# Norm 2's vectors loaded after gate/up's second chunk, and the cross heads' probabilities turned directly behind their scaling

## The chip, the cores and the metric

The kernel runs on one NeuronCore of a Trainium2 chip. The metric is device time in microseconds, the median of several executions of the same program. Before the change three executions took 380.92, 380.79 and 378.37 us, so the median is 380.79 us. One more execution was recorded by the profiler, and every row below is from it: it took 380.38 us.

## The reference

One decoder layer on 256 tokens of width 1024, in float32: a pooling mixer beside causal attention, then cross-attention of four heads of width 256 into 256 memory tokens, then a SwiGLU feed-forward of width 2816. A layer norm stands behind each of the three parts. What the change touches is the cross-attention and its norm:

```python
def memory_cross_attention(h, mem, w_xq, w_xkv, w_xo):
    q = (h @ w_xq).reshape(B_, S_, XATTN_HEADS, XATTN_HEAD_DIM)
    kv = mem @ w_xkv
    ...
    s = jnp.einsum('bshd,bmhd->bhsm', q, k, ...) * (XATTN_HEAD_DIM ** -0.5)
    p = jax.nn.softmax(s, axis=-1)
    o = jnp.einsum('bhsm,bmhd->bshd', p.astype(v.dtype), v).reshape(B_, S_, D)
    return o @ w_xo
...
    h = layer_norm(DEEPNORM_ALPHA * h + memory_cross_attention(h, mem, w_xq[l], w_xkv[l], w_xo[l]),
                   ln2_g[l], ln2_b[l])
```

## The kernel before

Every weight matrix is read once, in pieces of 512 KB, by one stream (class `Stream`). A piece lands in one of seven `raw` buffers, ACT copies it to a rounded tile `hi` (L99), and DVE subtracts to get the remainder `lo` (L100). TensorE then forms each product from three matmuls, hi·hi, hi·lo and lo·hi (L256 to L258, L274). All loads are issued from SP's queue in program order, and a load waits until the `raw` buffer that it fills has been split. `ws.before(number, load)` puts another load into that queue just ahead of piece `number`; norm 2's two vectors, `g` and `b` (512 KB each, one row of 4 KB repeated over 128 partitions, L224), stand there ahead of the first and the third piece of gate/up's first chunk.

The order of the instructions on each engine is the order in which the Python code is written. Generators such as `do_xq(h)` (the query product of head h, 16 steps of three matmuls) are advanced by `run(gen, n)`, and other calls are put between.

For each cross head h the path is:

- `xscores(h)`: the scores on TensorE into tile `xs` in PSUM; the row maximum (L440, DVE), the exponentials (L429, ACT), and the scaling by the sums (L434 and L436, DVE) give the probabilities `xpr`.
- `xprobs_out(h)`: DVE turns 32x32 blocks of `xpr` into a tile that is also called `xs` (L340), and POOL's queue issues one DMA of 256 KB that writes it to a DRAM tile `xd` (L343).
- `xprobs_in(h)`: POOL's queue issues four DMAs of 64 KB (L351) that read `xd` back, block rows exchanged, into `xr`. They wait for the write to land.
- `xprobs_split(h)`: ACT and DVE split `xr` into hi and lo, tile `xst` (L319, L320).
- `xattend(h)`: TensorE multiplies `xst` with the values `xv` into tile `xo` (L256 to L258).

Head 3 is turned on TensorE instead (`xprobs_pe`). The pieces below call these steps out(h), in(h) and split(h).

The tiles `xs` (of L340), `xr` and `xst` share one tag of the pool `small`, with three buffers. A new tile of the tag takes a buffer whose former tile is finished with by the code written so far, and its first writer then waits for that tile's last readers and writers:

```python
st = sp.tile([P, 4, n, 32], F32, name=f"{name}s", tag="pair", bufs=3)       # xs, in turned()
raw = sp.tile([P, 4, n, 32], F32, name=f"{name}r", tag="pair", bufs=3)      # xr, in landed()
st = sp.tile([P, 2, 2, S], F32R, name="xst", tag="pair", bufs=3)            # xst, in xprobs_split()
```

Behind the fourth head's scores comes the output product of the cross-attention (`project(c_xo, ...)`, tile `acc`), norm 2, and the gate/up product (tile `pg`).

Of the kernel before, what the change touches and what calls it, by code (L numbers as in the profile page):

```python
# [125 lines left out]
def decoder_layer(  # L126
# [18 lines left out]
    def bank(name):  # L145
        return pb.tile([P, 512], F32, tag="b", name=name)
# [5 lines left out]
    ws = Stream(nc, wp)  # L152
# [28 lines left out]
    c_gu = [ws.add(w_gu[c], 4) for c in range(NFC)]  # L181
# [39 lines left out]
    def load_norm(tag, i, v):  # L221
        def load():
            gb[tag, i] = nmp.tile([P, D], F32, tag=tag, name=f"{tag}{i}")
            nc.sync.dma_start(gb[tag, i], v[None, :].to_broadcast([P, D]))  # L224
        return load
# [1 line left out]
    ws.before(c_v[3][0], load_mem)  # L227
    ws.before(c_xk[1][0], load_pool)
    ws.before(c_mix[3][0], load_x)
    ws.before(c_gu[0][0], load_norm("g", 2, ln2_g))  # L230
    ws.before(c_gu[0][2], load_norm("b", 2, ln2_b))
    ws.before(c_dn[4][0], load_norm("g", 3, ln3_g))
    ws.before(c_dn[6][0], load_norm("b", 3, ln3_b))

# [18 lines left out]
    def three(ps, w, y, start, stop, part=False):  # L253

        (wa, wb), (ya, yb) = w, y
        nc.tensor.matmul(ps, wa, ya, start=start, stop=False, skip_group_check=part)  # L256
        nc.tensor.matmul(ps, wa, yb, start=False, stop=False, skip_group_check=part)  # L257
        nc.tensor.matmul(ps, wb, ya, start=False, stop=stop, skip_group_check=part)  # L258

    def pair(hl, *ix):  # L260
        return hl[0][ix], hl[1][ix]
# [48 lines left out]
    def run(gen, n=None):  # L310

        while n is None or n > 0:
            if next(gen, gen) is gen:
                return False
            n = None if n is None else n - 1
        return True
# [18 lines left out]
    def turned(blocks, n, name, queue=nc.sync):  # L335

        st = sp.tile([P, 4, n, 32], F32, name=f"{name}s", tag="pair", bufs=3)
        for at, src in blocks:
            m = src.shape[1]
            nc.vector.transpose(st[:, :, at:at + m, :].rearrange("p j m b -> p m j b"),  # L340
                                src.rearrange("p m (j b) -> p m j b", b=32))
        via = hp.tile([P, 4, n * 32], F32, name=f"{name}d")
        queue.dma_start(via, st.rearrange("p j m b -> p j (m b)"))  # L343
        return via

    def landed(via, n, name, queue=nc.sync, raw=None):

        if raw is None:
            raw = sp.tile([P, 4, n, 32], F32, name=f"{name}r", tag="pair", bufs=3)
        for j in range(4):  # L350
            queue.dma_start(raw[32 * j:32 * (j + 1)].rearrange("p i m b -> p i (m b)"),  # L351
                              via[:, j, :].rearrange("(i a) r -> a i r", i=4))
        return raw
# [72 lines left out]
    def exps(dst, src, mx, sign=1.0):  # L426
        sm = sp.tile([P, 2], F32, name="sm", bufs=6)
        for j in range(2):
            nc.scalar.activation(dst[:, j, :], src[:, j, :], AF.Exp, bias=mx[:, j:j + 1], scale=sign,  # L429
                                 accum_out=sm[:, j:j + 1])  # L430
        return sm

    def scaled(dst, sm):
        nc.vector.reciprocal(sm, sm)  # L434
        for j in range(2):
            nc.vector.tensor_scalar(dst[:, j, :], dst[:, j, :], sm[:, j:j + 1], None, op0=OP.mult)  # L436

    def negmax(src):
        mx = sp.tile([P, 2], F32, name="mx", bufs=6)
        nc.vector.tensor_reduce(mx, src, op=OP.max, axis=AX.X, negate=True)  # L440
        return mx
# [287 lines left out]
    def do_xq(h):  # L729
        ps = (bank if h == 0 else accbank)("pxq").rearrange("p (f t) -> p f t", f=2)  # L730
        yield from proj_t([ps[:, f, :] for f in range(2)], c_xq[h], h1T)
        xqT[h] = [sp.tile([P, 2, S], F32R, name=f"xq{i}", tag="pr", bufs=PR_BUFS) for i in range(2)]
        split_scaled(*xqT[h], ps, 256 ** -0.5)

    def xscores(h):
        ps = bank("xs").rearrange("p (t s) -> p t s", t=2)
        for t in range(T):
            for kk in range(2):
                three(ps[:, t, :], pair(xqT[h], ALL, kk, slice(t * P, (t + 1) * P)), pair(xkT, ALL, 2 * h + kk),
                      kk == 0, kk == 1)  # L740
        pr = sp.tile([P, 2, T, P], F32, name="xpr", tag="pr", bufs=PR_BUFS)
        by_t = pr.rearrange("p s t b -> p t s b")
        scaled(by_t, exps(by_t, ps.rearrange("p t (s b) -> p t s b", s=2), negmax(ps)))
        xpr[h] = pr

    def xprobs_out(h):
        turnsx[h] = turned([(0, xpr[h].rearrange("p s t b -> p (s t) b"))], 4, "x", nc.gpsimd)

    def xprobs_in(h):
        turnsx[h] = landed(turnsx[h], 4, "x", queue=nc.gpsimd)  # L750

    def xprobs_split(h):
        raw = turnsx[h].rearrange("p i m b -> p m i b")
        st = sp.tile([P, 2, 2, S], F32R, name="xst", tag="pair", bufs=3)
        xpt[h] = st[:, 0], st[:, 1]
        split(*[x.rearrange("p s (t i b) -> p (s t) i b", t=T, i=4) for x in xpt[h]], raw)
# [18 lines left out]
    xq = [do_xq(h) for h in range(XH)]  # L775
    run(xq[0])
    run(xq[1], 5)
    xscores(0)
    run(xq[1])
    xprobs_out(0)  # L780
    run(xq[2], 5)
    xscores(1)
    xprobs_in(0)
    run(xq[2])
    xprobs_out(1)
    run(xq[3], 5)
    xscores(2)
    xprobs_in(1)
    xprobs_split(0)
    run(xq[3])  # L790
    xprobs_out(2)

    h2 = ap.tile([P, T, D], F32, tag="a8", name="h2")
    xo = project(c_xo, lambda k: (oT[0][:, k], oT[1][:, k]), 4)
# [177 lines left out]
```

## Time and profile before

| what | value |
|---|---|
| median of three executions | 380.79 us (378.37 to 380.92) |
| profiled execution | 380.38 us |
| its span, first to last instruction | 378.6 us |
| mean granted TensorE clock | 0.993 |
| PE busy | 367.7 us (97%) |
| DVE busy | 262.2 us (69%) |
| ACT busy | 177.4 us (47%) |
| POOL busy | 34.7 us (9%) |
| DMA | 84.52 MB, mean 223 GB/s |

The profiler numbers everything from the span's start; 1.8 us of the profiled execution lie around the span. PE is TensorE's matmuls and PEld its weight loads, DVE is VectorE, ACT ScalarE, POOL GpSimd, SP SyncE. A bracket behind a row of the timeline gives how long the engine was idle ahead of it and what ended that. The granted clock is a share of TensorE's 2.4 GHz: 1.00, or 0.50 for 1.2 GHz. From issue to landing of a DMA is counted from the start of the instruction that issues it.

### The profile page before, as it was taken

Reading aid. Unit: us, or ns where it says so; the run is one execution under the profiler, and the core shown is the slowest. Engines: PE = TensorE matmul, PEld = TensorE weight load, DVE = VectorE, ACT = ScalarE, POOL = GpSimd, SP = SyncE. Lnnn points to the kernel's source line nnn. Section 1 sums busy time; section 2 is a strip of 40 time slices with the busy share of each in tenths; the row PEclk is TensorE's granted clock in tenths of the full one; section 3 lists DMA queues with packets and bytes.
Section 4 is the critical chain, followed back from the end, with each engine's and each line's share of the span. In section 5 each row is a group of like instructions: output and inputs, shape, how many; then the busy total and the mean of one; then the engine's idle time right before and its main releaser. Section 6 shows DMA issues by size and latency. Waiting matters only on the chain.

```text
span 378.6 us, 5525 instructions
## 1 busy us (share of the span) xinstructions
PE 367.7 (97%) x2024; PEld 317.6 (84%) x2024; DVE 262.2 (69%) x388; ACT 177.4 (47%) x259; POOL 34.7 (9%) x66
## 2 busy tenths in 40 slices
PE   9999999999999999899999999999999999999992
PEld 8997998997878999788878888888888888888881
DVE  4778899974698877465889765666665666353275
ACT  4756775653152944354138445454545454434000
POOL 1000157140110002320100000000000000000000
PEclk9999999999999999899999999999999999999998
DMA  7998699799337998544107998787879977730011
GB/s 236 412 412 298 190 341 307 261 251 367 124 111 234 392 312 265 150 155 161 56 2 264 353 308 256 243 238 250 237 230 316 279 241 251 206 106 0 0 51 62
DMA packets 32539, 84.52 MB, mean 223 GB/s; under 512 B 4096, under 2 KB 12160, under 8 KB 32384
## 3 DMA queue, kind: packets, MB, share of 16 engines
q1 hardware_dynamic: 30224, 79.05, 63.7%
q0 software_dynamic: 1712, 4.72, 4.2%
q10 hardware_dynamic: 576, 0.39, 0.3%
q8 instruction: 16, 0.26, 0.3%
q14 instruction: 11, 0.09, 0.1%
HBM read 76.81 MB, written 7.34 MB: 222 GB/s over the span
## 4 chain that ended last, share of the span: by engine, by line
PE 89%; DVE 4%; DMA 3%; issue 1%; ACT 1%; POOL 0%; SPq 0%; DVEq 0%
PE pg L258 10%; PE pg L257 10%; PE pg L256 10%; PE acc L256 9%; PE acc L257 9%; PE acc L258 9%; PE pxk L274 6%; PE pqk L392 6%; PE pxq L274 3%; PE pu L274 3%; PE xv L256 2%; PE xv L258 2%; PE xv L257 2%; DMA w61r<-in_w_gu 1%; PE pv L256 1%
## 5 line engine op out<-in xcount | busy, mean ns | idle before, releaser
L623 POOL TENSOR_TENSOR rs<-rs,mhalf 128x1 f32<-128x1 f32 x6 | 5.4, 897 | 231.4 <-DVE rs L622 231.4
L832 ACT ACTIVATE sg<-pg 128x256 f32<-128x256 f32 x22 | 8.4, 383 | 12.9 <-PE pg L258 12.8
L612 DVE SCALAR_TENSOR_TENSOR r<-h,acc 128x256 f32<-128x256 f32 (+1 forms) x10 | 5.1, 520 | 10.9 <-PE acc L258 10.9
L833 DVE TENSOR_TENSOR sg<-sg,pg 128x256 f32<-128x256 f32 x22 | 9.3, 421 | 4.0 <-ACT sg L832 2.6
L429 ACT ACTIVATE pr<-pr,mx 128x128 f32<-128x128 f32 (+1 forms) x16 | 7.1, 444 | 8.3 <-DVE mx L460 8.3
L351 POOL DMA_DIRECT2D pt<-pd x16 | 8.8, 555 | 6.6 <-DMA pd<-ps 4.1
L319 ACT CAST h2Th<-tp 128x512 fp32r<-128x512 f32 x4 | 2.3, 587 | 13.5 <-PE tp L330 13.4
L615 DVE BATCH_NORM_STATS2 st<-r 128x6 f32<-128x512 f32 (+1 forms) x14 | 8.1, 580 | 0.5
L320 DVE TENSOR_TENSOR gTl<-gr,gTh 128x512 fp32r<-128x512 f32 x11 | 7.5, 686 | 1.2 <-ACT gTh L319 1.2
L429 ACT ACTIVATE xpr<-xs,mx 128x256 f32<-128x256 f32 x8 | 3.7, 471 | 9.1 <-DVE mx L440 9.1
L319 ACT CAST gTh<-gr 128x512 fp32r<-128x512 f32 x11 | 6.8, 616 | 2.2 <-DMA gr<-gd 2.2
L628 DVE SCALAR_TENSOR_TENSOR r<-r,mv,g 128x512 f32<-128x512 f32 x11 | 7.8, 743 | 0.0
L340 DVE STREAM_TRANSPOSE gs<-sg 128x512 f32<-128x512 f32 x11 | 7.8, 705 | 0.0
L351 POOL DMA_DIRECT2D xr<-xd x12 | 6.5, 550 | 13.1 <-DMA w61r<-in_w_gu 5.4
L343 POOL DMA_DIRECT2D pd<-ps x4 | 2.5, 614 | 51.0 <-DVE ps L340 50.7
L256 PE MATMUL xo<-xst,xv 128*128 128x256 f32 x16 | 5.0, 314 | 1.5 <-ACT xst L319 1.5
L436 DVE TENSOR_SCALAR pr<-pr,sm 128x128 f32<-128x128 f32 (+1 forms) x16 | 6.2, 425 | 0.3
L434 DVE RECIPROCAL sm<-sm 128x2 f32<-128x2 f32 x12 | 2.0, 163 | 5.5 <-ACT xpr L429 4.4
L320 DVE TENSOR_TENSOR oTl<-xo,oTh 128x512 fp32r<-128x512 f32 x4 | 2.8, 692 | 4.2 <-ACT oTh L319 4.2
L634 DVE SCALAR_TENSOR_TENSOR h<-r,rs,b 128x512 f32<-128x512 f32 x8 | 5.6, 744 | 0.0
L319 ACT CAST oTh<-xo 128x512 fp32r<-128x512 f32 x4 | 2.3, 587 | 6.9 <-PE xo L258 6.9
L257 PE MATMUL xo<-xst,xv 128*128 128x256 f32 x16 | 5.1, 317 | 0.3 <-DVE xst L320 0.3
(1092 smaller groups left out, 1414.3 us busy)
## 6 DMA issues: line engine op xcount, KB each, us to landing
gd<-gs SPq DMA_DIRECT2D x11, 256.0 KB, 4.9
gr<-gd SPq DMA_DIRECT2D x44, 64.0 KB, 4.7
pd<-ps POOLq DMA_DIRECT2D x4, 384.0 KB, 4.9
pt<-pd POOLq DMA_DIRECT2D x16, 96.0 KB, 8.1
g<-in_ln_g SPq DMA_DIRECT2D x3, 512.0 KB, 6.1
b<-in_ln_b SPq DMA_DIRECT2D x3, 512.0 KB, 6.7
wr<-in_w_qkv SPq DMA_DIRECT2D x5, 256.0 KB, 5.4
mr<-in_mem_t SPq DMA_DIRECT2D x1, 1024.0 KB, 11.7
```

Of the source, the lines that this page charges most:

```text
L256: nc.tensor.matmul(ps, wa, ya, start=start, stop=False, skip_group_check=part)
L257: nc.tensor.matmul(ps, wa, yb, start=False, stop=False, skip_group_check=part)
L258: nc.tensor.matmul(ps, wb, ya, start=False, stop=stop, skip_group_check=part)
L274: nc.tensor.matmul(pss[f], w[:, s], y, start=k == 0 and f == 0 and n == 0, stop=k == KD - 1 and n == 2, skip_group_check=True)
L319: nc.scalar.copy(h, ps)
L320: nc.vector.tensor_sub(l, ps, r32(h))
L351: queue.dma_start(raw[32 * j:32 * (j + 1)].rearrange("p i m b -> p i (m b)"), via[:, j, :].rearrange("(i a) r -> a i r", i=4))
L392: nc.tensor.matmul(qk[i][:, f, :], w[:, c * P:(c + 1) * P], y, start=k == 0 and f == 0 and w is hi and y is x_hi, stop=k == KD - 1 and w i ...
L429: nc.scalar.activation(dst[:, j, :], src[:, j, :], AF.Exp, bias=mx[:, j:j + 1], scale=sign, accum_out=sm[:, j:j + 1])
L615: nc.vector.bn_stats(self.st[:, self.n, :], self.r[:, c0:c1])
L832: nc.scalar.activation(sg, ps[:, :CW].rearrange("p (f b) -> p f b", f=2), AF.Silu, bias=0.0, scale=1.0)
L833: nc.vector.tensor_mul(sg, sg, ps[:, CW:].rearrange("p (f b) -> p f b", f=2))
```

## The change

Three things move; no instruction is added or taken away. Norm 2's `g` and `b` are loaded ahead of the second and the third piece of gate/up's second chunk, w64 and w65, and no longer ahead of w59 and w61. out(0), out(1) and out(2) are written directly behind the scores of their head, rather than after the rest of a query product. in(0) and in(1) are written two steps ahead of the next head's scores, rather than behind them.

```diff
--- before.py
+++ after.py
@@ -227,8 +227,8 @@
     ws.before(c_v[3][0], load_mem)
     ws.before(c_xk[1][0], load_pool)
     ws.before(c_mix[3][0], load_x)
-    ws.before(c_gu[0][0], load_norm("g", 2, ln2_g))
-    ws.before(c_gu[0][2], load_norm("b", 2, ln2_b))
+    ws.before(c_gu[1][1], load_norm("g", 2, ln2_g))
+    ws.before(c_gu[1][2], load_norm("b", 2, ln2_b))
     ws.before(c_dn[4][0], load_norm("g", 3, ln3_g))
     ws.before(c_dn[6][0], load_norm("b", 3, ln3_b))
 
@@ -776,19 +776,21 @@
     run(xq[0])
     run(xq[1], 5)
     xscores(0)
+    xprobs_out(0)
     run(xq[1])
-    xprobs_out(0)
-    run(xq[2], 5)
+    run(xq[2], 3)
+    xprobs_in(0)
+    run(xq[2], 2)
     xscores(1)
-    xprobs_in(0)
+    xprobs_out(1)
     run(xq[2])
-    xprobs_out(1)
-    run(xq[3], 5)
+    run(xq[3], 3)
+    xprobs_in(1)
+    run(xq[3], 2)
     xscores(2)
-    xprobs_in(1)
+    xprobs_out(2)
     xprobs_split(0)
     run(xq[3])
-    xprobs_out(2)
 
     h2 = ap.tile([P, T, D], F32, tag="a8", name="h2")
     xo = project(c_xo, lambda k: (oT[0][:, k], oT[1][:, k]), 4)
```

On DVE's queue each turn into `xs` (L340) moves up to directly behind the scaling of its head (L436). For heads 0 and 1 it passes one weight remainder and one query remainder. For head 2 the piece of the queue was this (`xpr_1811` holds its probabilities, `xst_1825` is split(0), w57 a weight piece, `xq1` the query remainder of head 3; the brackets name semaphores):

```order
L436 TENSOR_SCALAR xpr_1811<-xpr_1811,sm_1814 128x2x128 [waits DVE_49]
L436 TENSOR_SCALAR xpr_1811<-xpr_1811,sm_1814 128x2x128
L320 TENSOR_TENSOR xst_1825<-xr_1724,xst_1825 128x512 [waits DMASW5_49,DMASW6_49,DMASW1_49,DMASW7_49,DMASW0_49,Activation_49]
L100 TENSOR_TENSOR w57l_1838<-w57r_1525,w57h_1837 128x1024 [waits DMAHW0_49,PE_49,Activation_49]
L324 SCALAR_TENSOR_TENSOR xq1_1868<-pxq_1776,xq0_1867 128x512 [waits Activation_49]
L340 STREAM_TRANSPOSE xs_1871<-xpr_1811 128x4x4x32 [waits DMASW3_49,DVE_49]
```

and now it is this (`xpr_1812` holds the probabilities of head 2):

```order
L436 TENSOR_SCALAR xpr_1812<-xpr_1812,sm_1815 128x2x128 [waits DVE_49]
L436 TENSOR_SCALAR xpr_1812<-xpr_1812,sm_1815 128x2x128
L340 STREAM_TRANSPOSE xs_1821<-xpr_1812 128x4x4x32 [waits DMASW1_49,DVE_49]
L320 TENSOR_TENSOR xst_1825<-xr_1692,xst_1825 128x512 [waits DMASW6_49,DMASW5_49,DMASW7_49,DMASW0_49,Activation_49]
L100 TENSOR_TENSOR w57l_1838<-w57r_1525,w57h_1837 128x1024 [waits DMAHW0_49,PE_49,Activation_49]
L324 SCALAR_TENSOR_TENSOR xq1_1870<-pxq_1772,xq0_1869 128x512 [waits Activation_49]
```

The turn of head 2 stood behind split(0), the weight and the query, and stands ahead of split(0) now. It has a new wait as well, for DMASW1: the names that begin with DMASW are eight semaphores on which the DMAs of POOL's queue count in turn, and here it is the count that out(1) brings.

On ACT's queue the order of the instructions stays the same, and what split(0) (`xst_1825`) waits for does not. Before:

```order
L99 CAST w56h_1777<-w56r_1496 128x1024 [waits DMAHW7_49]
L429 ACTIVATE xpr_1811,sm_1814<-xs_1798,mx_1812 128x2x128 [waits DVE_49]
L429 ACTIVATE xpr_1811,sm_1814<-xs_1798,mx_1812 128x2x128
L319 CAST xst_1825<-xr_1724 128x512 [waits DMASW6_49,DMASW5_49,DMASW7_49,DMASW1_49,DMASW0_49]
L99 CAST w57h_1837<-w57r_1525 128x1024 [waits DMAHW0_49,PE_49]
```

and now:

```order
L99 CAST w56h_1773<-w56r_1496 128x1024 [waits DMAHW7_49]
L429 ACTIVATE xpr_1812,sm_1815<-xs_1799,mx_1813 128x2x128 [waits DVE_49]
L429 ACTIVATE xpr_1812,sm_1815<-xs_1799,mx_1813 128x2x128
L319 CAST xst_1825<-xr_1692 128x512 [waits DMASW5_49,DMASW6_49,DMASW1_49,DMASW7_49,DMASW0_49,DVE_49]
L99 CAST w57h_1837<-w57r_1525 128x1024 [waits DMAHW0_49,PE_49]
```

What moved is a wait: split(0) of head 0 now waits for DVE, namely for the turn of head 2, and the count of DMASW6 that it waits for is the one that out(2) brings (before, the one that in(0)'s second read brings). DMASW1, for out(1), stands in both.

On SP's queue `g` passes five weight pieces and `b` four:

```order
-L224 DMA g_1590<-in_ln_g 128x1024
 L80 DMA w59r<-in_w_gu 128x1024
 L80 DMA w60r<-in_w_gu 128x1024
-L224 DMA b_1683<-in_ln_b 128x1024
 L80 DMA w61r<-in_w_gu 128x1024
 L80 DMA w62r<-in_w_gu 128x1024
 L80 DMA w63r<-in_w_gu 128x1024
+L224 DMA g_1841<-in_ln_g 128x1024
 L80 DMA w64r<-in_w_gu 128x1024
+L224 DMA b_1927<-in_ln_b 128x1024
 L80 DMA w65r<-in_w_gu 128x1024
```

What moved is the two norm loads alone; the weight pieces keep their order. On POOL's queue the order is the same as before: out(0), in(0), out(1), in(1), out(2), in(2).

## Rows read from the trace of the kernel before

**Rows 1.** Page, part 1: engine, busy us (share of the span), instructions.

```profile
PE 367.7 (97%) x2024; PEld 317.6 (84%) x2024; DVE 262.2 (69%) x388; ACT 177.4 (47%) x259; POOL 34.7 (9%) x66
```

**Rows 2.** Waits: engine, tile and line, releaser, us in total, times, longest.

```profile
PE xo L256 <- ACT xst L319: 1.5, 1, 1.5
```

**Rows 3.** Timeline of PE from 155: start, us, engine, line, operation, operands, count, [idle before].

```profile
155.05 0.28 PE L274 MATMUL pxq<-h1Tl,w50h 128*128 128x256 f32 x1
155.17 0.28 PE L274 MATMUL pxq<-h1Th,w50l 128*128 128x256 f32 x1
156.97 0.38 PE L256 MATMUL xo<-xst,xv 128*128 128x256 f32 x1 [1.53 <-ACT xst L319]
157.70 0.43 PE L257 MATMUL xo<-xst,xv 128*128 128x256 f32 x1 [0.34 <-DVE xst L320]
...
161.34 0.28 PE L256 MATMUL xs<-xkTh,xq 128*128 128x256 f32 x1
```

**Rows 4.** Windows of 1 us: busy of PE, PEld, DVE, ACT, POOL, granted clock, DMA.

```profile
158.00:159.00 1.00, 1.00 (x7) 1.00 (x7) 1.00 (x1) 0.37 (x1) 0.95 (x2) 0.50 0.41 119
...
161.00:162.00 1.00, 1.00 (x9) 1.00 (x9) 1.00 (x2) 0.41 (x1) 0.20 (x1) 0.84 0.81 320
```

**Rows 5.** Timeline of ACT, xst casts of heads 0 and 2.

```profile
156.31 0.62 ACT L319 CAST xst<-xr 128x512 fp32r<-128x512 f32 x1 [3.03 <-issue]
...
170.13 0.62 ACT L319 CAST xst<-xr 128x512 fp32r<-128x512 f32 x1
```

**Rows 6.** Timeline of POOL, out(0), in(0), out(1), in(1), out(2).

```profile
143.33 0.60 POOL L343 DMA_DIRECT2D xd<-xs  x1 [33.37 <-DVE xs L340]
149.35 2.18 POOL L351 DMA_DIRECT2D xr<-xd  x4 [5.41 <-DMA w61r<-in_w_gu]
151.51 0.56 POOL L343 DMA_DIRECT2D xd<-xs  x1
156.77 2.18 POOL L351 DMA_DIRECT2D xr<-xd  x4 [4.69 <-issue]
160.64 0.56 POOL L343 DMA_DIRECT2D xd<-xs  x1 [1.69 <-DVE xs L340]
```

**Rows 7.** Tile view, issue to landing: out(0), out(1), out(2), then in(0).

```profile
DMA to landing us min/median/max: 5.5/5.5/5.5
...
DMA to landing us min/median/max: 4.7/4.7/4.7
...
DMA to landing us min/median/max: 2.9/2.9/2.9
...
DMA to landing us min/median/max: 2.5/2.9/3.4
```

**Rows 8.** Timeline of DVE, heads 0 to 2 and norm 2.

```profile
139.11 0.62 DVE L436 TENSOR_SCALAR xpr<-xpr,sm 128x256 f32<-128x256 f32 x2
...
142.33 0.70 DVE L340 STREAM_TRANSPOSE xs<-xpr 128x512 f32<-128x512 f32 x1
...
146.31 0.62 DVE L436 TENSOR_SCALAR xpr<-xpr,sm 128x256 f32<-128x256 f32 x2
...
153.51 0.62 DVE L436 TENSOR_SCALAR xpr<-xpr,sm 128x256 f32<-128x256 f32 x2
...
185.22 1.40 DVE L628 SCALAR_TENSOR_TENSOR r<-r,mv,g 128x512 f32<-128x512 f32 x2
```

**Rows 9.** Timeline of SP's queue: norm loads and the weights beside them.

```profile
135.39 0.43 SPq L224 DMA_DIRECT2D g<-in_ln_g  x1
...
141.48 0.42 SPq L224 DMA_DIRECT2D b<-in_ln_b  x1
...
151.42 0.33 SPq L80 DMA_DIRECT2D w63r<-in_w_gu  x1
159.16 0.33 SPq L80 DMA_DIRECT2D w64r<-in_w_gu  x1
```

**Rows 10.** Tile view, issue to landing of norm 2's g.

```profile
DMA to landing us min/median/max: 6.1/6.1/6.1
```

## The prediction

> **What bounds the kernel now.** I began with the page's first part, the busy share of each engine [rows 1]. The reader is to see that PE is busy for 97% of the span, so that only a change of PE's work, or of the few places where PE stands, can move the end. The change adds no work to PE and takes none away. So the next view is the list of waits, for PE alone: its longest entry is a single wait of 1.5 us of `xo`, the first matmul of head 0's attention, for ACT's `xst`, which is split(0) [rows 2]. That place is where this change works.
>
> The timeline of PE shows what the place costs [rows 3]. PE issues a matmul of this shape every 0.12 us (155.05 to 155.17), so that the first `xo` could start at 155.29 and does so at 156.97: 1.68 us. The second, which needs the remainder from DVE, comes 0.73 us later where 0.12 would do: 0.61 us. From 157.70 to 161.34 PE then issues 17 matmuls in 3.64 us, 0.214 us each where 0.12 x 17 = 2.04 us would do: 1.60 us. The windows tell why: the granted clock is 0.50 there, 1.2 GHz, and comes back during 161 to 162 [rows 4]. It fell when the stall was over. The whole place costs 1.68 + 0.61 + 1.60 = 3.9 us.
>
> The last question is what split(0) waits for. ACT starts it at 156.31, and the row names no engine as releaser [rows 5]. Two DMA chains can be tried. The data: in(0) is issued by POOL from 149.35 for 2.18 us [rows 6], so that its fourth read is issued at 150.98 and lands at most 3.4 us later [rows 7], at 154.4. That is 1.9 us too early to be the releaser. The buffer: out(1) is issued at 151.51 [rows 6] and lands 4.7 us later [rows 7], at 156.21, and ACT starts 0.1 us behind it. POOL's in(1), which waits for the same landing, starts at 156.77. So split(0) is held by the landing of out(1), whose tile `xs` sat in the buffer that split(0) writes to. Its data had been there for two microseconds.
>
> **The change, part by part.** I take the buffers first, since everything hangs on them. The tag has three. When split(0)'s tile is asked for in the changed code, `xr` of head 0 (its source) and `xr` of head 1 (not yet split) are in use, and the third was last given to `xs` of head 2, because out(2) is now written ahead of split(0). So split(0) has to wait until out(2) has landed, where it waited for out(1). The order of ACT's queue shows it as a new wait for DVE, whose turn fills that tile. The turn of head 2 in its turn waits for out(1), whose buffer it takes over. The chain is now out(1) landed, turn of head 2, out(2) issued, out(2) landed, split(0). I follow it through.
>
> Head 0. Its scaling starts at 139.11 and takes 0.62 us [rows 8], so the turn can run from 139.8 to 140.5 instead of from 142.33. POOL starts an out 0.30 us behind its turn's end (142.33 + 0.70, then 143.33 [rows 6, 8]): 140.8. Nothing of the trace shows a landing at that moment without the norm loads; the nearest rows are the three landings of 2.9, 4.7 and 5.5 us [rows 7], and they are the bounds: out(0) lands between 143.7 and 146.3. POOL goes on 0.5 us later (143.33 + 5.5 = 148.83, then 149.35) and needs 2.18 us, so it is free between 146.4 and 149.0. The data of in(0) is in place by 151.9 at the latest, 2.5 us sooner than before or more.
>
> Head 1. The scaling starts at 146.31, and the turn ends at 147.7. POOL takes out(1) at 148.0, or at 149.0 where in(0) is late; before it was 151.51. It lands between 150.9 and 154.5, and POOL is through with in(1) between 153.6 and 157.2.
>
> Head 2. Here the gain of the heads before meets its limit: the scores stand where they stood, and the scaling starts at 153.51 [rows 8] whatever the DMAs did. The turn runs from 154.2 to 154.9. POOL takes out(2) at 155.2 at the soonest, at 157.2 if in(1) is late. Before it was 160.64, so out(2) moves up by up to 5.4 us, and still it is issued as late as PE already wants `xo` (155.29). It lands between 155.2 + 2.9 = 158.1 and 157.2 + 5.5 = 162.7. Split(0) starts 0.1 us later, at 158.2 to 162.8 against 156.31: **1.9 to 6.5 us later**, with no end on the gaining side.
>
> Which value? The 2.9 us are out(2)'s own of before, beside w64, issued at 159.16; the 5.5 us are out(0)'s, behind `b`, issued at 141.48 [rows 9]. In the changed queue `g` follows w63, which was issued at 151.42 [rows 9], some 4 us ahead of out(2), and it took 6.1 us in a busier stretch [rows 10], so that its tail at most is in out(2)'s way. That is nearest to the 2.9 row; I take 3.3 us and an out(2) at 155.2, which lands at 158.5. Split(0) starts at 158.6: +2.3 us.
>
> The Trainium skill ("DMA: Bandwidth & Descriptors", section "Anatomy of one DMA — SWDGE (gpsimd) path") fits a DMA of POOL's queue as 2.0 us and its bytes over 436 GB/s; by that 256 KB take an estimated 2.6 us, and the sum would be +1.6 us instead of +2.3. The trace has 2.9 us at its best and 5.5 at its worst for the same transfer, so the sum goes by the trace.
>
> The clock. The half-speed stretch of before cost 1.60 us. With a longer stall it can fall into the stall in part, and cost less, down to nothing (-1.6), or last on behind it, up to twice (+1.6). No row tells which; I leave it at 1.60, no change.
>
> The norm loads. `g` and `b` leave the stretch in which out(0) is under way. That makes out(0) land sooner, which head 2's scores make worthless, as shown. In their new place `g` is issued at about 151 and `b` behind w64. The first use of `g` is at 185.22 [rows 8], over 25 us after the 6.1 us of its load are over, and `b`'s follows at 186.6; I cost them at nothing there. On SP nothing waits behind them longer than the 0.43 us of an issue, and the weight pieces ahead of them come earlier. If that cover were gone, norm 2 would wait by as much as the load is late.
>
> The rest of the move. The three turns pass one weight remainder each on DVE, 0.7 us, which PE does not ask for at that time. On ACT the split of w57 and the query of head 3 stand behind split(0) and are late by the same 2.3 us, as is all of PE's work from `xo` on, so that they lose nothing against it. in(2) now waits for head 0's attention, whose buffer it takes over: 12 matmuls, of which the first takes 0.73 us and the others 0.214, end 3.1 us behind the first `xo`'s start, at 162.4, and with 0.5 us, 1.6 to the fourth read and 3.4 for that one its data is there by 167.9; split(2) was not started before 170.13 [rows 5].
>
> The sum against the profiled execution: 380.38 + 2.3 = **382.7 us**. That execution lies 0.4 us under the median of the three, 380.79. A measurement of this kernel can tell about 1% from no change, 3.8 us: faster is below 377.0, slower above 384.6.
>
> **The rivals.** *The stall closes.* Were split(0) given a buffer that is free, it would need only its data, there by 151.9, and ACT and DVE would be done with it before 155.29. All 3.9 us of the place go: 376.5. For it: the data is indeed sooner. Against it: three buffers, and the new wait in ACT's queue. Chance 0.06.
>
> *The loss is paid back by the clock.* The half-speed stretch falls within the longer stall: 382.7 - 1.6 = 381.1. Chance 0.10.
>
> *The norm load holds both writes.* `g` stands ahead of out(2) now as `b` stood ahead of out(0). If out(1) takes 5.5 us from 149.0, in(1) keeps POOL until 157.2, and an out(2) that takes 4.7 to 5.5 us lands at 161.9 to 162.7. Split(0) is then 5.7 to 6.5 us late, and the time is 386.1 to 386.9. It decides as soon as out(2) lands later than 160.4, since 4.2 us late is 384.6. For it: 5.5 us has been seen. Against it: the DMA engines are less busy past 155. Chance 0.16.
>
> *POOL cannot issue beside DVE.* Each out would then be held until the DVE instruction beside it ends; with 1.4 us, that of a pair of large ones [rows 8], for out(1) and out(2) this gives 2.3 + 2.8 = 5.1 us, 385.5. Against it: out(0), out(1) and out(2) took 0.60, 0.56 and 0.56 us to issue [rows 6], all with DVE at work. The Trainium skill ("SBUF — State Buffer", section "SBUF: two separate sides") states such a lock between VectorE and GpSimd's descriptor writing for some forms of instruction; by that rule the moved issues would be longer, and the trace shows none that is. Chance 0.02.
>
> **How the numbers follow.** The forecast has the rest, 0.66; its own range is 382.2 to 384.6 (1.9 us late to the 1% bound). The range of 8 in 10 reaches down to 380.5, under the clock's case, for a measured run may lie a little lower, and up to 386.2, into the case of the held writes. Faster: 0.06. Same: 0.66 + 0.10 = 0.76. Slower: 0.16 + 0.02 = 0.18.
>
> **What would show it.** In the changed profile the turns start near 139.8, 147.0 and 154.2, out(2) near 155.2, and split(0) starts 0.1 us behind out(2)'s landing, with in(0)'s data landed over 5 us ahead of it. PE's wait ahead of the first `xo` grows from 1.5 to about 3.8 us. I am wrong if split(0) starts ahead of out(2)'s landing, if out(2) lands before 157 or past 160.4, or if PE shows a new wait behind 165.

## The result, and the profile after

The changed kernel takes 383.12 us (median of 7 executions, 382.05 to 384.44), the kernel before in the same comparison 378.50 us (7 executions, 378.18 to 380.92). The ratio is 1.010 with a 95% interval of 1.007 to 1.013: slower, by 1.0% by this ratio and by 1.2% between the two medians. The profiled execution took 383.19 us, 2.81 us over that of before (380.38). Its span is 381.4 us.

The list of waits, for PE, has one entry that grew [rows 2]:

```profile
PE xo L256 <- ACT xst L319: 3.3, 1, 3.3
```

PE's timeline shows the same place [rows 3], with two later starts: the first matmul of the output product and the first one on weight piece w52.

```profile
155.02 0.28 PE L274 MATMUL pxq<-h1Th,w50l 128*128 128x256 f32 x1
158.64 0.58 PE L256 MATMUL xo<-xst,xv 128*128 128x256 f32 x1 [3.34 <-ACT xst L319]
159.37 0.58 PE L257 MATMUL xo<-xst,xv 128*128 128x256 f32 x1
...
164.44 0.63 PE L256 MATMUL acc<-w51h,oTh 128*128 128x512 f32 x1
...
169.06 0.40 PE L256 MATMUL acc<-w52h,oTh 128*128 128x512 f32 x1
```

The first `xo` now starts 3.62 us behind the last query matmul where it was 1.80 us, and the output product reaches w52 at 169.06. In the trace of before the last two rows read:

```profile
162.05 0.40 PE L256 MATMUL acc<-w51h,oTh 128*128 128x512 f32 x1
...
166.23 0.40 PE L256 MATMUL acc<-w52h,oTh 128*128 128x512 f32 x1
```

From the last query matmul to w52 it is 14.04 us after (169.06 - 155.02) and 11.06 us before (166.23 - 155.17 [rows 3]). The difference, 2.98 us, covers the 2.81 us by which the profiled times differ. I call this stretch **the crossing** below; it is the measure by which the experiments are compared.

What split(0) waits for is on ACT's timeline (head 0's split, then head 2's) [rows 5], on POOL's (out(0), in(0), out(1), in(1), out(2)) [rows 6], and in the landings of the three outs [rows 7]:

```profile
157.97 0.62 ACT L319 CAST xst<-xr 128x512 fp32r<-128x512 f32 x1 [4.84 <-DMA xd<-xs]
...
172.96 0.62 ACT L319 CAST xst<-xr 128x512 fp32r<-128x512 f32 x1
```

```profile
140.62 0.60 POOL L343 DMA_DIRECT2D xd<-xs  x1 [30.51 <-DVE xs L340]
144.07 2.18 POOL L351 DMA_DIRECT2D xr<-xd  x4 [2.85 <-DMA xd<-xs]
147.82 0.56 POOL L343 DMA_DIRECT2D xd<-xs  x1 [1.57 <-DVE xs L340]
150.91 2.17 POOL L351 DMA_DIRECT2D xr<-xd  x4 [2.53 <-DMA xd<-xs]
155.02 0.56 POOL L343 DMA_DIRECT2D xd<-xs  x1 [1.94 <-DVE xs L340]
```

```profile
DMA to landing us min/median/max: 2.9/2.9/2.9
...
DMA to landing us min/median/max: 2.6/2.6/2.6
...
DMA to landing us min/median/max: 2.8/2.8/2.8
```

out(2) is issued at 155.02 and lands 2.8 us later, at 157.82; split(0) starts at 157.97, and this time the row names the releaser, the DMA `xd`. Its data had been there since about 149.3: in(0) was issued from 144.07, and its fourth read, issued near 145.7, landed 3.6 us later. The turns on DVE [rows 8] and the norm loads on SP's queue [rows 9] are where the change puts them:

```profile
139.61 0.71 DVE L340 STREAM_TRANSPOSE xs<-xpr 128x512 f32<-128x512 f32 x1
...
146.81 0.71 DVE L340 STREAM_TRANSPOSE xs<-xpr 128x512 f32<-128x512 f32 x1
...
154.01 0.71 DVE L340 STREAM_TRANSPOSE xs<-xpr 128x512 f32<-128x512 f32 x1
```

```profile
151.40 0.43 SPq L224 DMA_DIRECT2D g<-in_ln_g  x1
...
161.20 0.42 SPq L224 DMA_DIRECT2D b<-in_ln_b  x1
```

The windows show the granted clock behind the stall [rows 4]:

```profile
158.00:159.00 1.00, 0.36 (x1) 0.29 (x1) 0.38 (x1) 1.00 (x2) 0.00 (x0) 0.75 0.00 0
159.00:160.00 1.00, 0.86 (x4) 0.64 (x4) 0.74 (x2) 1.00 (x2) 0.00 (x0) 0.50 0.00 0
164.00:165.00 1.00, 1.00 (x6) 0.90 (x5) 0.35 (x2) 0.00 (x0) 0.55 (x2) 0.50 1.02 414
165.00:166.00 1.00, 1.00 (x5) 0.79 (x4) 0.37 (x1) 0.59 (x3) 0.00 (x0) 0.83 0.83 217
```

It is at 0.50 from within 158 to 159 until 165 to 166, where it was from about 158 to 161.3 before.

### The profile page after: what moved, and what is told of

It is laid out like the page before. It is cut to its first block, busy times and chain, and to the rows that moved or that the text cites. A ratio compares the mean times of both kernels' runs of the same rounds, so it can differ in the third digit from the quotient of the medians.

```text
span 381.4 us, 5523 instructions
## 1 busy us (share of the span) xinstructions
PE 369.1 (97%) x2024; PEld 319.0 (84%) x2024; DVE 262.4 (69%) x388; ACT 177.6 (47%) x259; POOL 34.6 (9%) x66
## 4 chain that ended last, share of the span: by engine, by line
PE 81%; issue 11%; DVE 2%; DMA 2%; POOL 2%; ACT 0%; DVEq 0%; POOLq 0%; ACTq 0%
PE pg L258 10%; PE pg L257 10%; PE pg L256 10%; PE acc L256 9%; PE acc L257 9%; PE acc L258 9%; PE pxk L274 6%; PE pqk L392 6%; PE pu L274 3%; DMA xd<-xs 2%; PE busy L363 1%; PE pv L256 1%; POOL xr L351 1%; PE pv L257 1%; PE pv L258 1%
## 5 line engine op out<-in xcount | busy, mean ns | idle before, releaser
L256 PE MATMUL xo<-xst,xv 128*128 128x256 f32 x16 | 5.2, 326 | 3.3 <-ACT xst L319 3.3
L340 DVE STREAM_TRANSPOSE gs<-sg 128x512 f32<-128x512 f32 x11 | 7.7, 704 | 0.0
L256 PEld LDWEIGHTS xo<-xst,xv 128*128 128x128 f32 x16 | 3.6, 224 | 3.6 <-ACT xst L319 3.5
L436 DVE TENSOR_SCALAR pr<-pr,sm 128x128 f32<-128x128 f32 (+1 forms) x16 | 5.5, 391 | 0.3
```

## The experiments

Each experiment ran on a chip together with executions of the kernel before, and "ratio" is to these, with its 95% interval. The first experiment and the three below it shared one chip (median of before 379.21 us), the next four a second (377.45 us), and the last two a third (377.66 us), so times from different chips are compared with care.

**split(0) written ahead of out(2).** The order of two calls, so that split(0) gets the buffer of out(1) again:

```diff
     xscores(2)
-    xprobs_out(2)
     xprobs_split(0)
+    xprobs_out(2)
     run(xq[3])
```

> The changed kernel with split(0) written ahead of out(2), so that its tile takes the buffer of out(1) again; nothing else differs. Theory (the loss is the buffer: split(0) waits for out(2)'s landing): out(1) landed at 150.4 and in(0)'s data at about 148, so split(0) starts right behind the exponentials of head 2, at 153.1, and the first xo needs no wait at 155.14. The stall of 3.5 us and the half-speed stretch go; a wait of up to 0.7 us for the query remainder of head 3 may show ahead of its scores. Time 376.3 to 377.3, against 383.1 of the change and 378.5 of before. Rival 1 (the norm loads cost the time where they stand now): still near 383. Rival 2 (split(0) waits for its data): still near 383, with split(0) near 158.

Measured: 376.79 us (12 executions, 376.28 to 378.16), ratio 0.996 (0.992 to 0.999). ACT's split(0), then PE:

```profile
153.01 0.61 ACT L319 CAST xst<-xr 128x512 fp32r<-128x512 f32 x1
```

```profile
155.01 0.28 PE L274 MATMUL pxq<-h1Th,w50l 128*128 128x256 f32 x1
155.13 0.28 PE L256 MATMUL xo<-xst,xv 128*128 128x256 f32 x1
...
162.54 0.40 PE L256 MATMUL acc<-w52h,oTh 128*128 128x512 f32 x1
```

split(0) follows the exponentials of head 2, PE does not stand, and the crossing is 7.53 us. The order of two lines gives back the whole loss, with the norm loads where the change put them. That is against rivals 1 and 2 of the expectation.

**The turns alone.** The changed kernel with the loads back in their old places:

```diff
-    ws.before(c_gu[1][1], load_norm("g", 2, ln2_g))
-    ws.before(c_gu[1][2], load_norm("b", 2, ln2_b))
+    ws.before(c_gu[0][0], load_norm("g", 2, ln2_g))
+    ws.before(c_gu[0][2], load_norm("b", 2, ln2_b))
```

> The changed order of out and in, with norm 2's loads at their old places. Theory (buffer): out(2) is issued at 155.0 as in the change, and lands in 2.6 to 2.9 us, so split(0) starts near 157.9 and the time is 382.6 to 383.6. Rival 1 (norm loads): the loss is gone, 378 to 379.

Measured: 382.62 us (6 executions), ratio 1.011 (1.007 to 1.016). The wait stays without the moved norm loads, so they do not make it. POOL's out(2), ACT's split(0) and the first `xo`:

```profile
156.39 0.56 POOL L343 DMA_DIRECT2D xd<-xs  x1 [1.19 <-DVE xs L340]
```

```profile
158.88 0.62 ACT L319 CAST xst<-xr 128x512 fp32r<-128x512 f32 x1 [4.38 <-DMA xd<-xs]
```

```profile
159.55 0.58 PE L256 MATMUL xo<-xst,xv 128*128 128x256 f32 x1 [2.87 <-ACT xst L319]
```

This execution came to the place 1.4 us later than the profiled one of the change (last query matmul at 156.39), out(2) landed in 2.3 us, and split(0) followed it. The crossing is 12.07 us (156.39 to 168.46), 2.0 us less than in the change. Only 0.46 us of that is the wait (3.16 us from the last query matmul to the first `xo`, against 3.62). Most of it is that the half-speed stretch ends sooner, in the first of these two windows:

```profile
162.00:163.00 1.00, 1.00 (x7) 1.00 (x7) 0.30 (x1) 0.00 (x0) 0.00 (x0) 0.54 0.51 98
163.00:164.00 1.00, 1.00 (x10) 1.00 (x10) 0.36 (x1) 0.98 (x2) 0.72 (x2) 1.00 0.76 246
```

Why it is shorter here, behind a stall of nearly the same length, no run settles.

**The loads alone.** The kernel before with the opposite edit of those two lines.

> The kernel before with norm 2's loads moved as in the change, and nothing else. Theory: out(0) lands in about 2.9 us where it took 5.5, so POOL is free when the turn of head 1 is done and issues out(1) near 150.6 rather than 151.5; out(1) lands at 153.2 to 155.3, and split(0), which waits for out(1) here, starts by 155.4 rather than at 156.31. The stall shrinks to 0 to 0.8 us and the half-speed stretch does not come: 376.3 to 377.8, a gain on 378.5. Rival 1 (norm loads cost): 380 or more.

Measured: 376.67 us (12 executions, 376.18 to 378.27), ratio 0.995 (0.992 to 0.998). POOL's out(0), in(0), out(1), in(1):

```profile
142.97 0.60 POOL L343 DMA_DIRECT2D xd<-xs  x1 [33.07 <-DVE xs L340]
146.38 2.18 POOL L351 DMA_DIRECT2D xr<-xd  x4 [2.81 <-DMA xd<-xs]
150.23 0.56 POOL L343 DMA_DIRECT2D xd<-xs  x1 [1.67 <-DVE xs L340]
153.42 2.17 POOL L351 DMA_DIRECT2D xr<-xd  x4 [2.63 <-DMA xd<-xs]
```

in(0) starts 3.4 us behind out(0)'s issue where it took 6.0 [rows 6], out(1) is issued as soon as its turn is done, and in(1) starts at 153.42 rather than 156.77. split(0) starts at 152.96, and the crossing is 7.23 us (154.82 to 162.05), without a wait. This half of the change is a gain by itself, as expected.

**Products of the zero tile in the stall (8).** One line ahead of `xattend(0)` in the changed kernel, `keep_busy(8)`.

> The changed kernel with 8 extra products of the zero tile (16 matmuls of 0.22 us, 3.5 us) on TensorE just ahead of the first xo, where it stands idle for 3.6 us; they write a bank that nothing reads. It parts the wait from the clock. Theory (the place costs a wait of 3.5 + 0.6 us, and on top 24 matmuls and two wide ones at half speed behind it, about 2.7 us): the granted clock stays 1.00, split(0) starts where it did, and the time is 380.2 to 380.8. Rival 3 (the clock costs nothing measurable): 383 as in the change. Rival 4 (the extra matmuls are themselves in the way): above 383.

Measured: 382.20 us (6 executions, 380.89 to 383.40), ratio 1.010 (1.006 to 1.015): the expected 380.2 to 380.8 was missed, and the run decides nothing on the clock, since the dose was wrong. The 16 matmuls took 1.94 us, 0.12 each and not 0.22, 1.57 us of the stall stayed open, and the clock still fell, to 0.50 from 160 on. The crossing is 12.86 us (155.60 to 168.46).

**The kernel before once more**, for a second profile.

> The kernel before, unchanged, for a second profile: its runs beside the first experiments lie in groups, 376.3 to 377.9, 379.0 to 379.4 and 380.2 to 382.6 us. Theory: they are executions of one program in which out(1) lands in time, lands late, or lands late and is followed by half-speed matmuls. A profiled execution of the first group shows out(0) landing in under 4 us, out(1) issued at 150.6 or before, and no wait of the first xo; one of the last group shows the wait of 1.5 us as in the first profile. Rival: the groups come from elsewhere, and this place looks alike in both.

Measured: 378.18 us (10 executions, 376.19 to 381.69); the profiled one took 376.46 us. POOL's out(0), in(0), out(1), the landings of out(0) and out(1), ACT's split(0) and PE:

```profile
142.91 0.61 POOL L343 DMA_DIRECT2D xd<-xs  x1 [33.06 <-DVE xs L340]
147.54 2.18 POOL L351 DMA_DIRECT2D xr<-xd  x4 [4.02 <-DMA w61r<-in_w_gu]
150.17 0.56 POOL L343 DMA_DIRECT2D xd<-xs  x1 [0.46 <-DVE xs L340]
```

```profile
DMA to landing us min/median/max: 4.1/4.1/4.1
...
DMA to landing us min/median/max: 3.1/3.1/3.1
```

```profile
153.35 0.62 ACT L319 CAST xst<-xr 128x512 fp32r<-128x512 f32 x1 [0.49 <-DMA xr<-xd]
```

```profile
154.75 0.28 PE L274 MATMUL pxq<-h1Th,w50l 128*128 128x256 f32 x1
154.88 0.28 PE L256 MATMUL xo<-xst,xv 128*128 128x256 f32 x1
...
162.31 0.40 PE L256 MATMUL acc<-w52h,oTh 128*128 128x512 f32 x1
```

out(0) landed in 4.1 us, so that POOL was free when the turn of head 1 was done; out(1) went out at 150.17, landed at 153.27, and split(0) started 0.1 us later. (Its row names a read of in(0), but the last of these had landed by 153.0, 3.7 us behind its issue at 149.2.) PE did not stand, and the crossing is 7.56 us against 11.06 in the first profile. The difference of the two, 3.5 us, is most of the 3.9 us between their times (380.38 and 376.46). So the kernel before has executions with the stall and without it, and in these two profiles the landings decide which. Of 23 executions on the chip of the first experiments 10 lay under 378.5 us, 4 between 378.9 and 379.4, 8 from 380.2 to 381.4, and one at 382.59. The profile that I predicted from was one with the stall; no execution of the middle group was profiled, so what it does is not shown.

**out(2) alone moved up**, in the kernel before:

```diff
     xprobs_in(1)
+    xprobs_out(2)
     xprobs_split(0)
     run(xq[3])
-    xprobs_out(2)
```

> The kernel before with out(2) alone written ahead of split(0); out(0), in(0), out(1), in(1) and norm 2's loads stand as before. Theory (buffer): split(0) now waits for out(2), and out(2) for POOL, which is busy with in(1) until 155.7 or, with a late out(0), 158.9. It lands at 158.5 to 161.9, split(0) starts 0.1 us later, 2.2 to 5.6 us behind the 156.31 of before, and the time is 383 to 387, as slow as the change or slower, although nothing of the norm loads was moved. Rival 1 (the norm loads make the loss): as before, 376 to 381.

Measured: 384.49 us (4 executions, 382.74 to 386.88), ratio 1.019 (1.011 to 1.027). POOL's in(1) and out(2), then ACT's split(0):

```profile
155.53 2.17 POOL L351 DMA_DIRECT2D xr<-xd  x4 [4.06 <-issue]
157.69 0.56 POOL L343 DMA_DIRECT2D xd<-xs  x1
```

```profile
160.25 0.62 ACT L319 CAST xst<-xr 128x512 fp32r<-128x512 f32 x1 [6.79 <-DMA xd<-xs]
```

out(2) is 2.7 us later than in the change and split(0) follows it, 2.3 us later. The one moved call makes the loss by itself, and a later landing of out(2) goes with a larger one: the crossing is 15.30 us (155.35 to 170.65).

**14 products of the zero tile** in place of 8.

> The changed kernel with 14 products of the zero tile ahead of the first xo, so that TensorE is busy through the whole stall (28 matmuls; 16 of them took 1.94 us in the kernel with 8 products, 0.12 us each, which left 1.6 us of the stall open and a half-speed stretch behind it). They write a bank that nothing reads. Theory: the granted clock stays 1.00 behind the stall, the 26 matmuls that the change runs at half speed take some 2.7 us less, and the time is 2.2 to 2.8 us under the change's on the same chip. Rival 3 (the clock costs nothing): the same as the change.

Measured: 381.25 us (10 executions, 380.80 to 382.86), against 382.80 us (4 executions, 382.18 to 384.30) of the changed kernel on the same chip. PE's products and first `xo`, and two windows behind:

```profile
155.76 3.29 PE L363 MATMUL busy<-const-float32-0.0 128*128 128x128 f32 x28
159.44 0.38 PE L256 MATMUL xo<-xst,xv 128*128 128x256 f32 x1 [0.40 <-ACT xst L319]
```

```profile
159.00:160.00 1.00, 0.43 (x2) 0.19 (x1) 0.57 (x1) 1.00 (x2) 0.00 (x0) 1.00 0.00 0
...
161.00:162.00 1.00, 0.98 (x9) 0.77 (x7) 1.00 (x2) 0.22 (x1) 0.00 (x0) 1.00 0.00 0
```

The clock stays at 1.00, and the crossing is 12.08 us. The time falls by 1.55 us, which is less than the 2.2 to 2.8 expected. What I left out: at full speed the first `xo`s end before the query of head 3 has been split (ACT does it behind split(0)), and PE waits 0.27 us for it, and 0.40 us of the stall stayed open. So the clock's share is some 1.5 us here, by the medians (1.55) and by the crossings (13.61 - 12.08 = 1.53). With four executions on one side, and the two sets overlapping, the size is rough; that it costs nothing is refuted by the crossings.

**The changed kernel once more**, on that chip.

> The changed kernel, unchanged, as the base for the one with 14 products on the same chip, and for a second profile. 382 to 384, with split(0) starting behind out(2)'s landing near 157.9 and PE idle for over 3 us ahead of the first xo. Rival (the stall of the first profile was a rare one): the wait is shorter than 2 us here.

Measured: 382.80 us (4 executions, 382.18 to 384.30), against 377.45 us of the kernel before, ratio 1.015 (1.007 to 1.024). The wait of the first `xo` is 3.3 us again and the crossing 13.61 us (154.54 to 168.15). Both profiles of the change have the stall, and none of its 11 executions lies under 382 us.

**Four buffers.** `bufs=4` instead of 3 for the tag of `xs`, `xr` and `xst`, and `PR_BUFS = 5` instead of 6 to make room; order and loads are the change's.

> The changed kernel, order and loads untouched, with four buffers instead of three for the tag that xs, xr and xst share; to make room, the tag of the queries and probabilities has five instead of six. Theory (buffer): split(0) gets the buffer of xs of head 1, whose out(1) has landed by 150.5, so it starts at 153.1 and the first xo follows the last query matmul without a wait; 376.3 to 377.8, as the kernel with split(0) written first. Rival (the order of the turns itself, or the norm loads, cost the time): near 383.

Measured: 377.11 us (12 executions, 376.36 to 377.97), ratio 0.998 (0.995 to 1.001). ACT's split(0):

```profile
153.90 0.61 ACT L319 CAST xst<-xr 128x512 fp32r<-128x512 f32 x1
```

The first `xo` follows at 155.96 without a wait, and the crossing is 7.61 us (155.84 to 163.45). Nothing but numbers of buffers was changed, and the wait is gone. This and the first experiment give split(0) another buffer in two ways, and the wait goes; out(2) moved up alone gives it that of out(2), and the wait comes. So the cause is shown from both sides.

**split(0) first, loads at their old places.**

> The change's outs and ins with split(0) written ahead of out(2), and norm 2's loads at their old places: the early turns by themselves, without the new wait. Theory: out(0) is issued near 140.8 but lands in 4 to 5.5 us behind the norm load, out(1) near 149, landing at 152.3 to 154.7; split(0) starts at 153.1 to 154.8, before or just as the first xo is due, so the stall stays under 0.7 us: 376.3 to 378, without executions at 380. Rival (only the norm loads' move takes the late landings away): executions between 379 and 382 as in the kernel before.

Measured: 376.96 us (12 executions, 376.32 to 377.87), ratio 0.997 (0.994 to 0.9997). No execution lies above 378, while of 23 of the kernel before on this chip 5 lay from 380.1 to 381.65 and one at 382.38. The late landing of out(0) that I expected did not come: issued at 141.16, it landed in 2.7 us. In the profiled execution it was out(1) that landed late, 5.0 us behind its issue at 148.37, and still in time (landing, then ACT's split(0)):

```profile
DMA to landing us min/median/max: 5.0/5.0/5.0
```

```profile
153.57 0.61 ACT L319 CAST xst<-xr 128x512 fp32r<-128x512 f32 x1
```

So the early turns are worth the same as the moved loads, provided that split(0) does not wait for out(2). Either takes the late executions of before away, and both together (the first experiment) give no more: 376.79, 376.67 and 376.96 us. The crossing is 7.2 to 7.6 us in all of them, with no wait left in it. All three lie some 6 us under the change (382.80 and 383.12 us, on other chips), and each beats the kernel before on its own chip, by 0.3 to 0.5%.

## Why the prediction was right, and where it was off

**The buffer.** Right, and the step that carried the forecast. split(0) starts 0.15 us behind out(2)'s landing; giving it another buffer in two ways removes the loss, and moving out(2) up alone makes it.

**The issue times.** I had 140.8, 148.0 and 155.2 for the outs; they are 140.62, 147.82 and 155.02, all 0.18 us sooner because this execution came to the place 0.15 us sooner. That head 2's scores, not the DMAs, set out(2) was right.

**The landing of out(2).** I took 3.3 us between 2.9 and 5.5; it is 2.8, just under that range. So the wait grew by 1.82 us (3.62 - 1.80), not by 2.3. The Trainium skill's fit ("DMA: Bandwidth & Descriptors", section "Anatomy of one DMA — SWDGE (gpsimd) path") gave an estimated 2.6 us; the 2.8 us measured here are nearer to it than to the 3.3 that I took, and nearest to the best row of before, 2.9.

**The clock.** This is the term that was mis-sized: "I leave it at 1.60, no change". Half speed lasted to past 165 instead of 161.3. Behind the first `xo` PE needs 5.80 us to the output product where it needed 5.08 (162.05 - 156.97), and 4.62 us from there to w52 where it needed 4.18: 0.72 + 0.44 = 1.16 us more. It lay inside the bounds of 1.6 either way, and on the losing side, so the rival in which the clock pays back did not come in this execution, nor in the second profile of the change. It is not ruled out for this order: in the profile of the turns alone the two stretches are 4.73 and 4.18 us, 0.35 us less than before (159.55 to 164.28 to 168.46). The term varies from one execution or kernel to the next, and no run here shows what sets it. 1.82 + 1.16 = 2.98 us, and I had 2.3. That the wait came out 0.5 us smaller and the clock 1.2 us larger, so that the sum was off by 0.7 us only, is luck.

**The base.** I made the sum against one execution and read its 3.9 us at this place as the kernel's own. They are that execution's. The three runs of before, 378.37 to 380.92, already lay further apart than the sum, and I did not ask why. Against an execution without the stall (376.46 us, on another chip) the change costs 6.7 us, and between the medians of the seven runs it costs 4.6, twice the 2.3 of the sum. The forecast time holds because both profiles of the changed kernel are in the stall, and the profile of before happened to be of an execution that was in it too; that is luck as well. It also moved the verdict: 383.12 us lies within my "same", 377.0 to 384.6, which was drawn around 380.79, but against 378.50 us, or 377.45 us on the second chip, the change is slower by 1.0 to 1.5%, clear of noise.

**The norm loads.** Nothing on PE waits for them in their new place, as costed: PE's list of waits has no new entry. "Head 2's scores make worthless" what they free was right for the changed order alone; in the order of before the moved loads took the late executions away (376.67 against 379.21 us).

**The other rivals.** The loads held neither write (2.6 us for out(1) and 2.8 us for out(2)). POOL issued the outs in 0.60, 0.56 and 0.56 us, as before, beside the turns' neighbours on DVE; the lock that the Trainium skill states ("SBUF — State Buffer", section "SBUF: two separate sides") does not show in these rows either. split(2) started 2.8 us later than before, as all of PE's work did, and made no wait.

## What to carry to other kernels

When a step is moved up in a pool of few buffers, write down who asks for a buffer in the new order: a tile that used to take a buffer long free may now take that of the very step that was moved up, and its reader then waits for it. In the trace, compare the landing of the data with the start of the reader; a gap between them that the reader's own engine does not fill points to a buffer, and one more buffer or two exchanged lines tell. And before costing a stall that one profile shows, look whether the runs fall into groups, for the stall may not be in all of them.

## What the runs showed of the hardware

The same write of 256 KB to DRAM from POOL's queue took 2.3 to 5.0 us to land in the experiments and up to 5.5 in the first profile. The late ones had other loads beside them, but a load beside it does not make a write late each time: out(2) of the change, with `g` issued 3.6 us ahead of it, took 2.8 us, and out(1) of the last experiment, 6.0 us behind `b`, took 5.0. What decides is not shown. Two executions of the kernel before had 5.5 and 4.1 us for out(0), and 4.7 and 3.1 us for out(1) behind it. By the two together out(1) landed at 156.21 in one and at 153.27 in the other, and that decides whether TensorE stands; with the half-speed matmuls behind the stall the crossing is 3.5 us longer.

An idle TensorE can be held at full clock with products that nobody reads: 28 of them in 3.29 us kept the granted clock at 1.00 through a stall behind which it was at 0.50 for more than 6 us in both profiles of the change, and for some 3 us in that of the turns alone.
